# Hybrid mLSTM / sliding-window step: the last two row tiles in another order, the samples' decay on GpSimd, keys loaded ahead of queries

## The chip, the core and the metric

One core of a Trainium2 chip runs the whole program. The metric is the time of one execution on the device, in microseconds. The engines are TensorE (PE, with its weight loads as PEld), VectorE (DVE), ScalarE (ACT), GpSimd (POOL) and SyncE (SP), which issues most DMAs. Each engine works through its own list of instructions in order and waits on semaphores that other engines and DMAs raise.

## The reference, cut to what matters

One layer of a decoder for 1024 prompt rows (d = 1024) and 32 sample rows (8 sequences of 4 tokens). The input goes through an adaptive normalisation and one wide projection; two branches follow, a matrix memory (mLSTM, 4 heads) and a sliding-window attention (8 query heads, 2 key/value heads, window 128); gates merge them, an output product and a residual follow, then a normalisation of each row.

```python
# mLSTM, one chunk
C_new = decay[..., None, None] * C + jnp.einsum('bhs,bhsd,bhse->bhde', w_end, k, v)
n_new = decay[..., None] * n + jnp.einsum('bhs,bhsd->bhd', w_end, k)
...
u = jax.nn.sigmoid(gm) * (y_m @ w_mo) + jax.nn.sigmoid(ga) * (y_a @ w_ao)
x = x + gate * (u @ w_o)
...
# rmsnorm(yp, g_final), rmsnorm(ys, g_final)
y = xf * lax.rsqrt(jnp.mean(xf * xf, axis=-1, keepdims=True) + NORM_EPS) * g
```

All is in float32. For the samples, C is 128 x 128 for each of 8 sequences and 4 heads, and n one more column; the decay is one number for each sequence and head.

## The kernel before, in words

Every large product is made of three matmuls in a reduced float32 form (high by high, high by low, low by high), so each operand is split first: ACT casts the high part, DVE subtracts it to get the low part. The big products run as seven block products in place of eight (a scheme after Strassen), so sums and differences of blocks are made by DVE too.

The order of the work around the large products is planned when the program is written out. A class, Side, holds streams of smaller work: attention units (one for each of 4 query groups and 4 pairs of row tiles), memory heads, and the four sample heads. Each is a generator; where it yields, it names a number of microseconds of matmul time to wait and the PSUM banks it wants next, and Side takes it up again between matmuls. The matmuls, and most instructions of DVE and ACT, are held in the order in which they are written (Ordered, line 212); GpSimd and SP are ordered by the scheduler.

Three places matter here.

- **Attention unit** (unit, line 856). It loads queries (tile uqv, from the DRAM tensor qD), the keys of up to three row tiles (tile ukv, from kD) and values. A call of dma first writes out stores that are still due for the tensor it reads. Then come the scores (PSUM tile sc): the queries' slices are PE's weights, the keys are streamed.
- **Sample head** (sample_head, line 1205). For one head the eight sequences' C and n lie in three tiles Cs (three, three and two sequences of 129 columns). Matmuls into sn read them; then they are multiplied by the decay (line 1261, in sxb); matmuls into sU make the update, and DVE adds it to Cs. Columns 128 of Cs go back to n by GpSimd. Meanwhile the large products use the PSUM tiles bw, bx, by and bz in turn; zt is one of the gate tiles made from bx.
- **The end** (lines 2240 to 2332). The output product runs over four blocks of two row tiles (256 rows). For a block, the seven products go to the PSUM tiles X, Z, W and Y (foX, foZ, foW, foY in the trace). The splits of the seven left operands are u3wh and u3wl for the last block. xb holds two rows of residuals, tile 6 and tile 7 in the last block; all of them are slices of two large tiles that the trace calls rows_h and rows_l, and so are g_final (gf, with its sign turned) and the samples' rows (x8, y8). add_row adds a product to a slice of xb; square (ACT, with a sum of its output) gives the sums of squares, one column of ss (fss) for a half or quarter row; norm_sum adds the columns up and scales them (fv); root_recip makes the negative reciprocal root: a square root on ACT, then a reciprocal and one Newton step on DVE (fy, fw). weighted multiplies by g_final, rows_out scales by the root and stores to y_p. In the last block the two halves of Y are separate PSUM tiles of 256 columns, so that their additions can start sooner. A row tile of 128 x 1024 goes out as two stores of 256 KB.

Of the kernel before, what the change touches and what calls it, by code (L numbers as in the profile page):

```python
# [20 lines left out]
D = 1024  # L21
SEQ = 1024
NB = 8
# [150 lines left out]
def body(tc, a):  # L174
    nc = tc.nc
    with ExitStack() as ctx:
# [20 lines left out]
        def sm(shape, name, bufs=3, dt=F32):  # L197
            return sp.tile(shape, dt, tag=name, bufs=bufs, name=name)
# [55 lines left out]
        def dma(out, in_, late=False):  # L254
            stores(in_.tensor)
            issue(out, in_, late)
# [599 lines left out]
        def unit(g, b0):  # L856
# [3 lines left out]
            qv, kv_ = ht([128, 4, 128], "uqv"), ht([128, 4, 128], "ukv")  # L860
            q, kT = qv[:, 0:2].rearrange("p c e -> p (c e)"), kv_[:, 0:3].rearrange("p c e -> p (c e)")
            vn = kv_[:, 3], qv[:, 2], qv[:, 3]
            dma(q, qD[g][:, b0 * 128:b0 * 128 + 256])
            dma(kT[:, n0 * 128:], kD[:, (b0 - 1 + n0) * 128:(b0 + 2) * 128])
            dma(qv[:, 2:4], vnD[:, b0:b0 + 2])
            if b0:
                dma(vn[0], vnD[:, b0 - 1])
# [337 lines left out]
        def sample_head(h):  # L1205
# [52 lines left out]
                mm(num[j:j + 32], qf[:, b * NS:(b + 1) * NS], Cs[b // 3][:, b % 3], start=(b < 4), stop=(b >= 4 and j > 0))  # L1258
            mm(num[:NS], z[:, 257:289], z[:, 128:257], start=False, stop=True)
            S.copy(ns4, num)  # L1260
            for c, b, m in zip(Cs, bs, ns_):
                V.tensor_tensor(c[:, :m], c[:, :m], sxb[:, h, 2, b].unsqueeze(2).to_broadcast((128, m, 129)), op=ALU.mult)
            yield 4.0, "ob"
            for i, (c, b, m) in enumerate(zip(Cs, bs, ns_)):
                up = (pb, pb, po)[i]([128, 388], f"sU{h}_{i}")
# [868 lines left out]
        def row_start():  # L2134
            if order_out:
                i, n = order_out.pop(0)
                blocks_of_rows[i].start(n)
# [26 lines left out]
        def residual(tb):  # L2164
            xb = misc[3 + tb % 4]
            dma(xb, a["x_prompt"][tb * 128:tb * 128 + 128], tb < 4)
            return xb
# [12 lines left out]
        def norm_rows(ss, m, parts):  # L2180

            return root_recip(norm_sum(ss, m, parts), m)
# [13 lines left out]
        def square(x, ss):  # L2196
            S.activation(pb([128, 512], "sq")[:x.shape[0], :x.shape[1]], x, AF.Square, accum_out=ss)
# [42 lines left out]
        for i, r in enumerate(blocks_of_rows):  # L2240
            nxt = i < 3
            aside = lambda *when: next(rows8, None) if i in when else None
            before, xb, ss = (xb, ss), [residual(2 * i + c) for c in range(2)], sm([128, 6], "fss", 2)
            if not i:
                weights_out(len(wo_parts))
            X, Z = pg([128, 512], "foX"), pa([128, 512], "foZ")
            row_start()
            r.product(1, X, True)
            if i == 3:
                sum8 = pb([128, 512], "fo8s")[:, :1]  # L2250
                for j in range(4):
                    mm(sum8[32 * j:32 * j + 32], cst[:, C_S32:C_S32 + 32], sq8, start=True, stop=True, share=4)
            W = copied(X, "foW", pg, new=r.w[1] if i == 0 else None)
            if i:
                add_row(before[0][1], lo, Y[0])
            row_start()
            r.product(5, Z, True)
            if i == 3:
                V.memset(before[1][:, 5:6], 0.0)
                V.tensor_copy(before[1][:, 4:5], sum8)  # L2260
            if i:
                square(before[0][0][:, hi], before[1][:, 1:2])
                square(before[0][1][:, lo], before[1][:, 2:3])
                if not nxt:
                    for c, x in ((lo, 0), (hi, 1), (hi, 0), (lo, 1)):
                        weighted(before[0][x], c)
                rs = norm_rows(before[1], 2 if nxt else 3, 2)
            for x in xb:
                add_row(x, hi, Z)
            row_start()  # L2270
            r.product(6, W, False)
            parts = ((0, 512),) if nxt else ((0, 256), (256, 256))
            Y = [copied(W, f"foY{c0}", pb if c0 else pa, slice(c0, c0 + n), r.w[6] if c0 or i == 0 else None) for c0, n in parts]
            aside(1, 2)
            for c in range(2) if i else ():
                rows_out(2 * i - 2 + c, before[0][c], rs[:, c:c + 1], V if nxt else None)
            row_start()
            r.product(2, X, False)
            add_row(xb[0], lo, X)
            square(xb[0][:, lo], ss[:, 0:1])  # L2280

            def seventh():
                for y, (c0, n) in zip(Y, parts):
                    r.product(7, y, False, c0, n)
                    add_row(xb[1], slice(512 + c0, 512 + c0 + n), y)

            def first_row():
                r.product(3, W, False)
                add_row(xb[0], hi, W)

            if nxt:
                seventh()
                row_start()
                square(xb[1][:, hi], ss[:, 3:4])
                first_row()
                row_start()
                aside(0, 1, 2)
                if not i:
                    dma(gf, a["g_final"].to_broadcast((128, D)))
                    S.activation(gf, gf, AF.Copy, scale=-1.0)  # L2300
                elif i == 1:
                    dma(gs8, gsD)
                    for j in range(4):
                        dma(gf8[32 * j:32 * j + 32], a["g_final"][:, 256 * j:256 * j + 256].to_broadcast((32, 256)))
                    dma(x8, a["x_sample"])
                else:
                    S.activation(gf8, gf8, AF.Copy, scale=-1.0)
                row_start()
                r.product(4, Y[0], False)
            else:  # L2310
                first_row()
                V.scalar_tensor_tensor(y8, x8, rs[:, 2:3], gf8, op0=ALU.mult, op1=ALU.mult)
                issue(a["y_s"], y8)
                square(xb[0][:, hi], ss[:, 1:2])
                seventh()
                rs = norm_rows(ss, 1, 2)
                square(xb[1][:, hi], ss[:, 2:3])
                rows_out(6, xb[0], rs)
                y7 = ht([128, 512], "foy7")
                for f, (y, (c0, n)) in enumerate(zip(Y, parts)):  # L2320
                    r.product(4, y, False, c0, n)
                    c = slice(c0, c0 + n)
                    if f:
                        weighted(xb[1], hi)
                        half = norm_sum(ss[:, 2:4], 1, 2)
                        add_row(xb[1], c, y)
                        V.tensor_tensor_reduce(y7[:, c], xb[1][:, c], xb[1][:, c], 1.0, 0.0, ALU.mult, ALU.add, accum_out=ss[:, 4:5])
                        V.scalar_tensor_tensor(half, ss[:, 4:5], 0.5 / D, half, op0=ALU.mult, op1=ALU.add)
                    else:
                        add_row(xb[1], c, y)  # L2330
                        square(xb[1][:, c], ss[:, 3:4])
        rows_out(7, xb[1], root_recip(half, 1), S)


OUTS = {
# [72 lines left out]
```

## Time and profile before

| | |
|---|---|
| median of 3 runs | 820.4 us (820.26 to 821.0) |
| the profiled execution's own time | 821.22 us |
| its span, first to last instruction | 819.4 us |
| mean granted TensorE clock | 0.996 |
| last matmul to the end of the span | 7.8 us, in which DVE is busy 3.6 and ACT 1.4 |
| busy: PE / DVE / ACT / POOL | 804.3 / 603.0 / 418.8 / 48.7 us |
| DMA | 165.51 MB, mean 202 GB/s |

The span is what the trace shows. The time of an execution has some 1.8 us more around it. A row of the time line reads: start and length in us, engine, line, operation, output tile <- input tiles, shapes, how many were merged, and in brackets how long the engine had been idle and what ended that. Line 220 is the helper through which most DVE, ACT and POOL instructions go, so tiles tell more than lines. Where an operation's record overlaps the next one's start by some 0.08 us, the engine had begun the next while the last one's output drained.

### The profile page before, as it was taken

The numbers are of one execution on the slowest core, as the hardware profiler recorded it, in microseconds if no ns is written. First come the engines' busy times: TensorE is split into PE (matmuls) and PEld (weight loads), VectorE is DVE, ScalarE is ACT, GpSimd is POOL, SyncE is SP. The second block draws the span as 40 slices with busy tenths as digits, with TensorE's granted clock in tenths as the row PEclk, the third lists the DMA queues.
The fourth block names the chain that finished last, engine by engine and source line by source line (L and its number), as shares of the span: only waits on it lengthen the run. The fifth ranks groups of instructions, "written<-read, shape, count | busy, mean of one in ns | idle before, by whom it ended". The sixth has DMA issues, their size and how long they took to land. (4 is left out here: it accounts for less than half of the span.)

```text
span 819.4 us, 15145 instructions
## 1 busy us (share of the span) xinstructions
PE 804.3 (98%) x5162; PEld 667.4 (81%) x5162; DVE 603.0 (74%) x1518; ACT 418.8 (51%) x1021; POOL 48.7 (6%) x121
## 2 busy tenths in 40 slices
PE   8999999999999999999999999999999999999996
PEld 5779898888788878888888888788888779997775
DVE  4899886755755557475668889898668997876666
ACT  5664356655565564546556555554446652224334
POOL 0120000010000000000001011010002101000000
PEclk9999999999999999999999999999999999999999
DMA  9993856646545424537764685764436689647632
GB/s 353 363 348 113 252 158 217 175 151 218 172 140 163 130 85 153 164 140 241 253 214 152 236 264 192 260 213 143 145 106 210 199 304 376 234 145 275 206 104 110
DMA packets 113475, 165.51 MB, mean 202 GB/s; under 512 B 21185, under 2 KB 55745, under 8 KB 113365
## 3 DMA queue, kind: packets, MB, share of 16 engines
q1 hardware_dynamic: 107172, 152.74, 56.3%
q10 hardware_dynamic: 4752, 7.60, 2.5%
q0 software_dynamic: 1472, 4.20, 1.3%
q8 instruction: 41, 0.67, 0.4%
q14 instruction: 38, 0.30, 0.1%
HBM read 115.51 MB, written 50.00 MB: 202 GB/s over the span
## 5 line engine op out<-in xcount | busy, mean ns | idle before, releaser
L220 ACT ACTIVATE p<-p,nmx 128x256 f32<-128x256 f32 (+1 forms) x64 | 31.1, 486 | 18.9 <-DVE nmx L220 17.9
L220 DVE CUSTOM_DVE_ANT_0 p<-sc,cst,sink 128x256 f32<-128x256 f32 (+1 forms) x64 | 26.1, 463 | 9.1 <-PE sc L275 9.0
L275 PE MATMUL g_aq<-h_h,wh_aq 128*128 128x384 f32 (+1 forms) x96 | 32.4, 337 | 0.1
L275 PE MATMUL g_aq<-h_h,wl_aq 128*128 128x384 f32 (+1 forms) x96 | 30.9, 322 | 0.0
L275 PE MATMUL g_aq<-h_l,wh_aq 128*128 128x384 f32 (+1 forms) x96 | 30.8, 321 | 0.0
L275 PE MATMUL g_w_mo<-ym_l,wh_w_mo 128*128 128x384 f32 (+1 forms) x96 | 30.8, 321 | 0.0
L275 PE MATMUL g_w_mo<-ym_h,wh_w_mo 128*128 128x384 f32 (+1 forms) x96 | 30.8, 321 | 0.0
L275 PE MATMUL g_w_mo<-ym_l,wl_w_mo 128*128 128x384 f32 (+1 forms) x96 | 30.8, 321 | 0.0
L220 DVE COPY p<-pt 128x512 f32<-128x512 f32 (+1 forms) x16 | 10.5, 656 | 15.2 <-PE pt L280 15.2
L220 ACT CAST wosh<-wor 128x512 fp32r<-128x512 f32 x24 | 14.8, 621 | 13.1 <-DVE wor L220 12.3
L275 PEld LDWEIGHTS g_aq<-h_h,wh_aq 128*128 128x128 f32 x96 | 18.0, 188 | 2.8 <-issue 1.5
L261 POOL DMA_DIRECT2D oD<-uqv x16 | 8.9, 553 | 179.6 <-ACT uqv L220 164.1
L220 DVE TENSOR_TENSOR wosl<-wor,wosh 128x512 fp32r<-128x512 f32 x24 | 16.5, 686 | 3.9 <-ACT wosh L220 3.2
L275 PE MATMUL sc<-ukv,uqv 64*128 64x256 f32 (+1 forms) x128 | 18.0, 390 | 0.9 <-DMA ukv<-kD 0.9
L220 DVE SCALAR_TENSOR_TENSOR tgw_mo<-tgw_mo,g_w_mo 128x384 f32<-128x384 f32 (+1 forms) x24 | 12.4, 518 | 8.6 <-PE g_w_mo L275 6.4
L275 PEld LDWEIGHTS g_w_mo<-ym_l,wh_w_mo 128*128 128x128 f32 x96 | 18.0, 188 | 0.0
L275 PEld LDWEIGHTS g_aq<-h_l,wh_aq 128*128 128x128 f32 x96 | 18.1, 188 | 0.0
L275 PEld LDWEIGHTS g_w_mo<-ym_h,wh_w_mo 128*128 128x128 f32 x96 | 18.0, 188 | 0.0
L275 PEld LDWEIGHTS g_w_mo<-ym_l,wl_w_mo 128*128 128x128 f32 x96 | 18.0, 188 | 0.0
L275 PEld LDWEIGHTS g_aq<-h_h,wl_aq 128*128 128x128 f32 x96 | 18.0, 188 | 0.0
L220 DVE TENSOR_TENSOR et<-et,S 128x384 f32<-128x384 f32 (+1 forms) x12 | 6.1, 509 | 15.0 <-PE S L275 15.0
L275 PE MATMUL g_mq<-h_h,wh_mq 128*128 128x384 f32 (+1 forms) x48 | 16.7, 349 | 0.3 <-ACT mk L220 0.3
(2065 smaller groups left out, 2819.7 us busy)
## 6 DMA issues: line engine op xcount, KB each, us to landing
early_h<-w_ada SPq DMA_DIRECT2D x8, 512.0 KB
adar_ga<-w_ada SPq DMA_DIRECT2D x16, 256.0 KB
wr_ga<-w SPq DMA_DIRECT2D x16, 256.0 KB
wr_gm<-w SPq DMA_DIRECT2D x16, 256.0 KB
taD<-gt SPq DMA_DIRECT2D x16, 256.0 KB
tmD<-gt SPq DMA_DIRECT2D x16, 256.0 KB
wor<-w_out SPq DMA_DIRECT2D x16, 256.0 KB
tga<-taD SPq DMA_DIRECT2D x16, 256.0 KB
```

Of the source, the lines that this page charges most:

```text
L220: ins = f(*args, **kw)
L261: ins = (eng or nc.sync).dma_start(out, in_)
L275: in_order(nc.tensor.matmul(out, lhsT, rhs, start=start, stop=stop, skip_group_check=more))
```

## The change

The queries' and keys' loads of an attention unit trade places. The samples' decay becomes eight operations on GpSimd, one for each sequence (128 x 129, with one number for each partition), in place of three on DVE. At the end, the last block's second half is written out in another order: the split of the last left operand comes behind the addition of X; tile 6 is weighted on DVE before its root is known and scaled on ACT (scaled_half) in place of one DVE operation that did both; half of product 7 and a weighting stand between tile 6's root on ACT and its reciprocal; tile 7's four sums of squares and a constant column (EPS times D) are added by one reduction, and the root is taken from that sum, with half of it over D computed beside the root.

```diff
@@ unit
+            dma(kT[:, n0 * 128:], kD[:, (b0 - 1 + n0) * 128:(b0 + 2) * 128])
             dma(q, qD[g][:, b0 * 128:b0 * 128 + 256])
-            dma(kT[:, n0 * 128:], kD[:, (b0 - 1 + n0) * 128:(b0 + 2) * 128])
             dma(qv[:, 2:4], vnD[:, b0:b0 + 2])
@@ sample_head
             S.copy(ns4, num)
-            for c, b, m in zip(Cs, bs, ns_):
-                V.tensor_tensor(c[:, :m], c[:, :m], sxb[:, h, 2, b].unsqueeze(2).to_broadcast((128, m, 129)), op=ALU.mult)
+            for b in range(NB):
+                c = Cs[b // 3][:, b % 3]
+                G.tensor_scalar(c, c, sxb[:, h, 2, b:b + 1], None, op0=ALU.mult)
             yield 4.0, "ob"
@@ the blocks of rows
-            row_start()
+            if nxt:
+                row_start()
             r.product(2, X, False)
             add_row(xb[0], lo, X)
-            square(xb[0][:, lo], ss[:, 0:1])
+            if nxt:
+                square(xb[0][:, lo], ss[:, 0:1])
 
-            def seventh():
-                for y, (c0, n) in zip(Y, parts):
+            def seventh(ps=(0, 1)):
+                for y, (c0, n) in list(zip(Y, parts))[ps[0]:ps[-1] + 1]:
                     r.product(7, y, False, c0, n)
                     add_row(xb[1], slice(512 + c0, 512 + c0 + n), y)
...
-            else:
-                first_row()
-                V.scalar_tensor_tensor(y8, x8, rs[:, 2:3], gf8, op0=ALU.mult, op1=ALU.mult)
-                issue(a["y_s"], y8)
-                square(xb[0][:, hi], ss[:, 1:2])
-                seventh()
-                rs = norm_rows(ss, 1, 2)
-                square(xb[1][:, hi], ss[:, 2:3])
-                rows_out(6, xb[0], rs)
-                y7 = ht([128, 512], "foy7")
-                for f, (y, (c0, n)) in enumerate(zip(Y, parts)):
-                    r.product(4, y, False, c0, n)
-                    c = slice(c0, c0 + n)
-                    if f:
-                        weighted(xb[1], hi)
-                        half = norm_sum(ss[:, 2:4], 1, 2)
-                        add_row(xb[1], c, y)
-                        V.tensor_tensor_reduce(y7[:, c], xb[1][:, c], xb[1][:, c], 1.0, 0.0, ALU.mult, ALU.add, accum_out=ss[:, 4:5])
-                        V.scalar_tensor_tensor(half, ss[:, 4:5], 0.5 / D, half, op0=ALU.mult, op1=ALU.add)
-                    else:
-                        add_row(xb[1], c, y)
-                        square(xb[1][:, c], ss[:, 3:4])
-        rows_out(7, xb[1], root_recip(half, 1), S)
+
+        def scaled_half(tb, x, c, r):
+            S.activation(x[:, c], x[:, c], AF.Copy, scale=r)
+            issue(a["y_p"][tb * 128:tb * 128 + 128, c], x[:, c])
+
+        def rest_of_seventh():
+            weighted(xb[0], hi)
+            seventh((1,))
+            square(xb[1][:, 768:1024], ss[:, 3:4])
+
+        V.scalar_tensor_tensor(y8, x8, rs[:, 2:3], gf8, op0=ALU.mult, op1=ALU.mult)
+        issue(a["y_s"], y8)
+        row_start()
+        square(xb[0][:, lo], ss[:, 0:1])
+        first_row()
+        square(xb[0][:, hi], ss[:, 1:2])
+        weighted(xb[0], lo)
+        seventh((0,))
+        square(xb[1][:, 512:768], ss[:, 2:3])
+        V.memset(ss[:, 6:7], EPS * D)
+        r6 = root_recip(norm_sum(ss, 1, 2), 1, rest_of_seventh)
+        scaled_half(6, xb[0], hi, r6)
+        r.product(4, Y[0], False, 0, 256)
+        add_row(xb[1], slice(0, 256), Y[0])
+        square(xb[1][:, 0:256], ss[:, 4:5])
+        scaled_half(6, xb[0], lo, r6)
+        weighted(xb[1], hi)
+        r.product(4, Y[1], False, 256, 256)
+        add_row(xb[1], slice(256, 512), Y[1])
+        y7 = ht([128, 512], "foy7")
+        V.tensor_tensor_reduce(y7[:, 0:256], xb[1][:, 256:512], xb[1][:, 256:512], 1.0, 0.0, ALU.mult, ALU.add, accum_out=ss[:, 5:6])
+        v = sm([128, 3], "fv", 2)
+        V.tensor_reduce(v[:, 0:1], ss[:, 2:7], op=ALU.add, axis=AX.X)
+        r7, w = (sm([128, 4], n, 2)[:, :1] for n in ("fy", "fw"))
+        S.activation(r7, v[:, 0:1], AF.Sqrt, scale=1.0 / D)
+        V.tensor_scalar(v[:, 1:2], v[:, 0:1], 0.5 / D, None, op0=ALU.mult)
+        V.reciprocal(r7, r7)
+        V.scalar_tensor_tensor(w, r7, v[:, 1:2], r7, op0=ALU.mult, op1=ALU.mult)
+        V.scalar_tensor_tensor(r7, w, 1.5, r7, op0=ALU.subtract, op1=ALU.mult)
+        rows_out(7, xb[1], r7, S)
```

More of the change, by code (lines that the diff above doesn't have):

```diff
@@ L2242, in body @@
             aside = lambda *when: next(rows8, None) if i in when else None
-            before, xb, ss = (xb, ss), [residual(2 * i + c) for c in range(2)], sm([128, 6], "fss", 2)
+            before, xb, ss = (xb, ss), [residual(2 * i + c) for c in range(2)], sm([128, 7], "fss", 2)
             if not i:
```

## The prediction, made before the result was known

> **What bounds the kernel now.** I read the page first, then the waits of PE, then the end of the time line, engine by engine.
>
> ```profile
> span 819.4 us, 15145 instructions
> PE 804.3 (98%) x5162; PEld 667.4 (81%) x5162; DVE 603.0 (74%) x1518; ACT 418.8 (51%) x1021; POOL 48.7 (6%) x121
> ```
>
> PE is busy 98% of the span, so an edit on another engine pays only in two ways: it shortens a wait of PE, or it shortens the stretch after the last matmul. The view of waits (who waited for whom: us in total, times, longest) lists what PE lost to others. After the start-up these two are the longest:
>
> ```profile
> PE bx L275 <- DVE zt L220: 1.3, 1, 1.3
> PE sc L275 <- DMA ukv<-kD: 0.9, 1, 0.9
> ```
>
> The change touches both: the samples' decay stood ahead of zt on DVE, and ukv is the tile that the keys are loaded into. What else it touches is the end. Here is the time line from the last matmul on (start, length, engine):
>
> ```profile
> 811.31 0.28 PE L275 MATMUL foY<-wosh,u3wl 128*128 128x256 f32 x1
> ...
> 810.41 1.42 DVE L220 SCALAR_TENSOR_TENSOR rows_h<-rows_h,fy,rows_l 128x512 f32<-128x512 f32 x2
> 811.74 0.41 DVE L220 TENSOR_TENSOR rows_h<-rows_h,foY 128x256 f32<-128x256 f32 x1
> 812.08 0.69 DVE L220 TENSOR_TENSOR rows_h<-rows_h,rows_l 128x512 f32<-128x512 f32 x1
> ...
> 813.01 0.41 DVE L220 TENSOR_TENSOR rows_h<-rows_h,foY 128x256 f32<-128x256 f32 x1
> 813.46 0.42 DVE L220 CUSTOM_DVE_ANT_0 foy<-rows_h 128x256 f32<-128x256 f32 x1
> 813.93 0.16 DVE L220 SCALAR_TENSOR_TENSOR fv<-fss,fv 128x1 f32<-128x1 f32 x1
> 814.36 0.16 DVE L220 RECIPROCAL fy<-fy 128x1 f32<-128x1 f32 x1 [0.27 <-ACT fy L220]
> 815.00 0.75 DVE L220 SCALAR_TENSOR_TENSOR rows_h<-rows_h,fy,rows_l 128x512 f32<-128x512 f32 x1
> ```
>
> The last matmul ends at 811.59, but its sum is added only at 813.01: DVE was still busy scaling row tile 6 (810.41), weighting tile 7 (812.08) and adding partial sums (to 813.01). So 1.4 us of the tail are DVE's queue, not arithmetic that needs the last product. From 813.01 to the end all is one chain.
>
> **Term 1, the last two row tiles.** DVE's rows from the scaling of tile 6 on; rows_h holds both tiles, foY the last products' two halves. Before:
>
> ```order
> L220 SCALAR_TENSOR_TENSOR rows_h_8801<-rows_h_8801,fy,rows_l_8800 128x512 x2
> L220 TENSOR_TENSOR rows_h_8801<-rows_h_8801,foY_9418 128x256
> L220 TENSOR_TENSOR rows_h_8801<-rows_h_8801,rows_l_8800 128x512
> L220 TENSOR_SCALAR fv<-fss 128x1
> L220 SCALAR_TENSOR_TENSOR fv<-fss,fv 128x1
> L220 TENSOR_TENSOR rows_h_8801<-rows_h_8801,foY_9420 128x256
> L220 ISA foy_9508,fss<-rows_h_8801 128x256
> L220 ISA fss 128x1
> L220 SCALAR_TENSOR_TENSOR fv<-fss,fv 128x1
> ```
>
> and now:
>
> ```order
> L220 TENSOR_TENSOR rows_h_8821<-rows_h_8821,foY_9438 128x256
> L220 TENSOR_TENSOR rows_h_8821<-rows_h_8821,rows_l_8820 128x512
> L220 TENSOR_TENSOR rows_h_8821<-rows_h_8821,foY_9440 128x256
> L220 ISA foy_9562,fss<-rows_h_8821 128x256
> L220 ISA fss 128x1
> L220 TENSOR_REDUCE fv<-fss 128x1
> L220 TENSOR_SCALAR fv<-fv 128x1
> ```
>
> The two scalings of tile 6 have gone to ACT, the partial sums to one reduction behind the last square; only the weighting of tile 7 stands between the two additions. The weightings of tile 6 that replace the scalings on DVE moved up, into gaps:
>
> ```profile
> 803.52 0.68 DVE L220 TENSOR_TENSOR u3wl<-u_h,u3wh 128x512 fp32r<-128x512 f32 x1
> 805.65 0.69 DVE L220 TENSOR_TENSOR u3wl<-u_l,u3wh 128x512 fp32r<-128x512 f32 x1 [1.45 <-ACT u3wh L220]
> 806.26 0.68 DVE L220 TENSOR_TENSOR rows_h<-rows_h,foX 128x512 f32<-128x512 f32 x1
> 806.86 0.68 DVE L220 TENSOR_TENSOR rows_h<-rows_h,foW 128x512 f32<-128x512 f32 x1
> 807.46 0.47 DVE L220 SCALAR_TENSOR_TENSOR rows_l<-rows_l,fy 128x256 f32<-128x256 f32 x1
> 808.75 0.42 DVE L220 TENSOR_TENSOR rows_h<-rows_h,foY 128x256 f32<-128x256 f32 x1 [0.48 <-PE foY L275]
> ```
>
> A 512-wide DVE operation takes a slot of 0.60 (806.26 to 806.86). In the new order the addition of X (0.60) and the samples' output (0.40) fill the 1.45 us hole before 805.65. From there I step through: the addition of W at 806.26, a weighting at 806.86, first half of product 7 at 807.46, partial sums to 808.3, the other weighting to 808.9, second half of 7 to 809.25 (its matmuls end at 808.71), root of tile 6 done about 809.85. The first half of product 4 is added when PE ends it, 810.2, the weighting of tile 7 runs to 811.2, and DVE is idle when the last matmul ends. The last addition then starts 0.04 behind PE, as at 808.75 (matmuls to 808.71): at 811.63 instead of 813.01. Gain: **1.38 us**.
>
> Behind it the chain stays as long: addition, square, its read-out, one small DVE operation (a reduction over five columns in place of a 0.16 us operation, 813.93), root on ACT, reciprocal. The new 0.5/D product stands ahead of the reciprocal, but beside the root: 0.20 after the reduction against 0.43 from 813.93 to 814.36. It costs nothing while that cover lasts, 0.2 without it. ACT takes on two scalings:
>
> ```profile
> 812.25 0.39 ACT L220 ACTIVATE sq<-rows_h 128x256 f32<-128x256 f32 x1 [1.90 <-DVE rows_h L220]
> 814.12 0.20 ACT L220 ACTIVATE fy<-fv 128x1 f32<-128x1 f32 x1 [1.36 <-DVE fv L220]
> 815.00 0.72 ACT L220 ACTIVATE rows_h<-rows_h,fy 128x512 f32<-128x512 f32 x1 [0.68 <-DVE fy L220]
> ```
>
> At 0.72 each, with a square between: 809.9, 810.6 (square, read-out), 811.1 to 811.8. The root of tile 7 wants ACT at about 812.75, so 0.9 us of room. Bounds of this term: 1.38 if so, about 0.5 if ACT runs a whole scaling late. The store of tile 6 leaves SP at 811.9, about as before (behind 811.8), so the last store has the queue to itself.
>
> **Term 2, the samples' decay on GpSimd.** Only the third head's decay stands before a wait of PE. DVE and PE there:
>
> ```profile
> 526.03 0.68 DVE L220 TENSOR_TENSOR wl_pquery_gate__6563<-wr_az,wh_pquery_gate__6562 128x512 fp32r<-128x512 f32 x1
> 526.77 0.68 DVE L220 TENSOR_TENSOR ws<-wr_az,wr_az 128x512 f32<-128x512 f32 x1
> 527.58 1.36 DVE L220 TENSOR_TENSOR Cs<-Cs,sxb 128x387 f32<-128x387 f32 x3
> 528.86 0.68 DVE L220 TENSOR_TENSOR wr_az<-wr_az,wr_az 128x512 f32<-128x512 f32 x1
> 529.46 0.67 DVE L220 SCALAR_TENSOR_TENSOR zt<-zt,bx 128x512 f32<-128x512 f32 x1
> ...
> 525.12 0.62 PE L275 MATMUL sn<-Cs,qd 128*32 128x129 f32 x16
> 530.19 0.50 PE L275 MATMUL bx<-h_h,wh_pquery_gate__6469 128*128 128x512 f32 x1 [1.30 <-DVE zt L220]
> 532.39 0.63 PE L275 MATMUL sU<-vm,skn 96*128 96x388 f32 x3
> ```
>
> PE wants the bank bx back and waits 1.30 for zt. The three decays take 527.58 to 528.86, 1.28 us. But the scheduler put another operation ahead of zt. Before, from the two small sums on:
>
> ```order
> L220 TENSOR_TENSOR gts<-gts,osm 128x32 x2
> L220 TENSOR_TENSOR Cs_0_6339<-Cs_0_6339,sxb 128x387
> L220 TENSOR_TENSOR Cs_1_6340<-Cs_1_6340,sxb 128x387
> L220 TENSOR_TENSOR Cs_2_6341<-Cs_2_6341,sxb 128x258
> L220 TENSOR_TENSOR wr_az_0_6405<-wr_az_0_6401,wr_az_0_6405 128x512
> L220 SCALAR_TENSOR_TENSOR zt<-zt,bx 128x512
> ```
>
> and now:
>
> ```order
> L220 TENSOR_TENSOR gts<-gts,osm 128x32 x2
> L220 TENSOR_TENSOR wr_az_0_6415<-wr_az_0_6411,wr_az_0_6415 128x512
> L220 TENSOR_TENSOR wr_az_0_6411<-ws_6573,wr_az_0_6411 128x512
> L220 SCALAR_TENSOR_TENSOR zt<-zt,bx 128x512
> L220 TENSOR_TENSOR zt<-zt,ho 128x512
> ```
>
> So zt gains 1.28 and loses 0.60: 0.68. From this comes off what GpSimd, now at work at the same time, takes from DVE. The trace has such pairs:
>
> ```profile
> 35.09 0.24 POOL L220 CAST h_h<-small 128x64 fp32r<-128x64 f32 x1
> 20.94 0.62 POOL L220 CAST wh_av<-wr_av 128x512 fp32r<-128x512 f32 x1
> 621.47 1.40 POOL L220 TENSOR_TENSOR yat3l<-yr,yat3h 128x512 fp32r<-128x512 f32 x1 [3.15 <-ACT yat3h L220]
> ...
> 35.10 0.77 DVE L220 TENSOR_TENSOR h_l<-x,h_h 128x512 fp32r<-128x512 f32 x1 [0.23 <-ACT h_h L220]
> 621.75 1.66 DVE L220 TENSOR_TENSOR wr_mo<-wr_mo,wr_mo 128x512 f32<-128x512 f32 x1
> ```
>
> A DVE operation on two SBUF tensors takes 0.68 alone, 0.77 beside a one-input GpSimd operation of 64 columns, 1.66 beside a two-input one of 512. GpSimd's decay is one-input, 129 columns; scaled by columns from the first pair (0.08 for 64), 0.16 a meeting, and as little as 0, as much as 0.98 by the second. From about 525.6 to zt I count three full-size two-input operations that can be delayed (behind 526.03, behind 526.77, the second wr_az): 0.48. What is left is **0.20 us**, between 0.68 (no meeting costs) and a loss. The Trainium skill (GPSIMD Engine Reference, 4.1 Engine selection) calls one-input work on GpSimd roughly line-rate, which at that page's 1.2 GHz makes an estimate of 0.11 for 129 columns: three meetings at that price would take 0.33, and the whole prediction would be 818.35 in place of 818.5. The row above (0.77 against 0.69) says dearer, and I keep to it.
>
> Length on GpSimd: by the two casts about 0.30 for 129 columns, eight make 2.4, and with a DVE operation waited out each time about 5.5. From 525.6 that ends by 531.1, before the sum with sU (532.39). The other three heads' decays stand before no listed wait of PE, so I give them nothing.
>
> **Term 3, keys' loads first.** SP's queue at the first attention unit, as a piece of the difference:
>
> ```order
> -L261 DMA qD_114<-aqr 128x384 x2
> +L261 DMA qD_114<-aqr 128x384
> +L261 DMA ukv<-kD 128x256
> +L261 DMA qD_114<-aqr 128x384
>  L261 DMA qD_114<-aqr 128x256
>  L261 DMA uqv<-vnD 128x256
>  L261 DMA uqv<-qD_114 128x256
> -L261 DMA ukv<-kD 128x256
> ```
>
> ```profile
> SPq L261 <- DMA qD<-aqr: 3.3, 1, 3.3
> ...
> 84.37 1.42 SPq L261 DMA_DIRECT2D qD<-aqr  x3
> 89.72 0.32 SPq L261 DMA_DIRECT2D uqv<-qD  x1
> 90.09 0.42 SPq L261 DMA_DIRECT2D ukv<-kD  x1
> 92.34 0.93 PE L275 MATMUL sc<-ukv,uqv 64*128 64x128 f32 x8 [0.89 <-DMA ukv<-kD]
> ```
>
> SP holds the queries' load until the first store of the queries has landed (the wait of 3.3); the keys' load, which needs none of that, stood behind it, 0.37 later, and PE waited for it. Now it goes out five us early and the queries' load is last. Its own time doesn't move (the first store stays ahead of it), so with an equal flight PE starts 0.37 sooner. Between 0 (if the queries landed as late) and 0.89; I take **0.35**. In the other fifteen units no such wait is listed, so nothing.
>
> **The sum.** 1.38 + 0.20 + 0.35 = 1.93 us: the profiled execution's span goes from 819.4 to 817.5, its time by the same step from 821.2 to 819.3. The three runs have a median of 820.4, so I predict **818.5**. PE's later waits are round trips that begin at PE, so they move along.
>
> **Rivals.** A: only the tail pays; GpSimd's meetings eat the 0.68 and the queries land no sooner: 820.4 - 1.38 = 819.0. For it: the measured 0.77 and 1.66; against it: three meetings must cost 0.23 each. B: the meetings cost nothing: 820.4 - 1.38 - 0.68 - 0.35 = 818.0; for it, that a decay may fall beside work that reads PSUM, as zt does. C: the tail gives little, because ACT reaches the last root a scaling late: 820.4 - 0.5 - 0.55 = 819.35; against it, 0.9 us of room. D, the slower side: DVE's meetings with GpSimd before zt. GpSimd runs eight decays from 525.6 on, and if each DVE operation on two SBUF tensors in that stretch (the three, and the small sums counted as two) waits as long as in the two-input pair, 0.98, zt comes 4.9 - 0.68 = 4.2 later and PE with it: 820.4 - 1.73 + 4.2 = 822.9. Five meetings turn the whole change into a loss from 0.48 each. The page named above states the cause as well (1. Specifications: the SBUF interfaces are shared, with contention against instructions with two SBUF inputs), without a price, and the 1.66 agrees. Against D: GpSimd's one-input cast over 512 columns takes 0.62 in all, and a decay is a quarter as wide.
>
> **Chances.** Forecast (818.1 to 818.9) 0.50; A 0.20; B 0.13; C 0.11; D 0.06. What can't be told from no change is 0.2%, 1.6 us: faster means below 818.76, slower above 822.0. The forecast's case lies below that line in 0.45 of its 0.50, B wholly, A in 0.05: faster 0.63. Same: the rest of A and of the forecast, C, and the milder meetings of D: 0.33. Slower 0.04, the rest of D. Range 817.7 to 819.6: it leaves out D and the edges of B and C.
>
> **What would show it.** Tail: the last addition on DVE within 0.1 us of the last matmul's end, two ACT scalings ending before the last root, and some 7.8 - 1.4 = 6.4 us from the last matmul to the end. Decay: bx waits about 1.1 instead of 1.30, DVE's wl and ws rows around GpSimd's decays lengthened by 0.1 to 0.2. Keys: sc waits about 0.5, on uqv. I'm wrong if DVE rows there stretch to a microsecond, if ACT's square or scaling ends behind 812.7, or if PE finds a new wait.

## The result, and the profile after

| | before | after |
|---|---|---|
| median | 821.04 us (22 runs, 820.08 to 824.11) | 818.85 us (22 runs, 817.71 to 820.05) |
| ratio after / before | | 0.9971, 95% interval 0.9965 to 0.9977 |
| profiled execution, its span | 821.22, 819.4 us | 820.05, 818.3 us |
| the same two kernels later, beside other runs | 821.48 us (22 runs) | 818.59 us (10 runs), ratio 0.9965 (0.9954 to 0.9976) |

The change made the kernel 2.4 us faster by the ratio (0.0029 of 821.04; interval 1.9 to 2.9) and 2.2 by the two medians. Forecast were 818.5 us and 1.93 us of gain, reckoned from a median of 820.4 over three runs of the kernel before; over 22 runs that median is 821.04. So the time lies in the range and the sign is right. The gain is some 0.4 us larger than the sum gave, and the time is still 0.35 us above the forecast, since the kernel before is 0.6 us slower than was taken. By the line that the prediction drew at 818.76, 0.2% under 820.4, the time of 818.85 is just on the side of no change; beside the 821.04 measured with it, it is 0.29% shorter. The profiled execution of the change happens to be the slowest of its 22. Its span is only 1.1 us shorter than before's, and that needs an explanation of its own.

The view of PE's waits after the change (who waited for whom: us in total, times, longest), from the places that the prediction spoke of and one that it didn't:

```profile
PE sc L275 <- DMA uqv<-qD: 1.6, 1, 1.6
PE bx L275 <- DVE zt L220: 1.0, 1, 1.0
PE foW L275 <- DVE u0wl L220: 0.5, 1, 0.5
```

The wait of sc is now ended by the queries (uqv) and not by the keys, but it has grown from 0.89 to 1.55. The wait of bx has shrunk from 1.30 to 0.99. The wait of foW for u0wl, at 743 us, is new.

The time line of the end after the change:

```profile
809.86 0.72 ACT L220 ACTIVATE rows_h<-rows_h,fy 128x512 f32<-128x512 f32 x1
...
810.66 0.69 DVE L220 TENSOR_TENSOR rows_h<-rows_h,rows_l 128x512 f32<-128x512 f32 x1
...
811.25 0.71 ACT L220 ACTIVATE rows_h<-rows_h,fy 128x512 f32<-128x512 f32 x1
...
811.44 0.28 PE L275 MATMUL foY<-wosh,u3wl 128*128 128x256 f32 x1
...
811.75 0.42 DVE L220 TENSOR_TENSOR rows_h<-rows_h,foY 128x256 f32<-128x256 f32 x1 [0.41 <-PE foY L275]
812.21 0.43 DVE L220 CUSTOM_DVE_ANT_0 foy<-rows_h 128x256 f32<-128x256 f32 x1
812.56 0.08 DVE L220 DVE_READ_ACCUMULATOR2_ANT fss<- 128x1 f32 x1
812.75 0.16 DVE L220 TENSOR_REDUCE fv<-fss 128x1 f32<-128x5 f32 x1
812.94 0.20 ACT L220 ACTIVATE fy<-fv 128x1 f32<-128x1 f32 x1 [0.98 <-DVE fv L220]
...
813.17 0.17 DVE L220 RECIPROCAL fy<-fy 128x1 f32<-128x1 f32 x1
...
813.82 0.75 DVE L220 SCALAR_TENSOR_TENSOR rows_h<-rows_h,fy,rows_l 128x512 f32<-128x512 f32 x1
```

The last addition starts 0.03 us behind the last matmul's end (811.72), and DVE had been idle 0.41 us before it: nothing but PE holds it up. From the start of the last matmul to the start of the last scaling it is 2.38 us; before it was 3.69 (811.31 to 815.00). The two scalings of tile 6 on ACT end at 811.96, and ACT is then idle 0.98 us until the last root. From the last matmul's end to the end of the span, the last store included, it is 6.6 us; before it was 7.8, and 6.4 was forecast.

DVE, GpSimd and PE around zt in the third head:

```profile
525.03 6.59 POOL L220 TENSOR_SCALAR Cs<-Cs,sxb 128x129 f32<-128x129 f32 x8 [18.25 <-PE sn L275]
...
525.46 0.68 DVE L220 TENSOR_TENSOR wl_pquery_gate__6578<-wr_az,wh_pquery_gate__6577 128x512 fp32r<-128x512 f32 x1
...
526.20 0.78 DVE L220 TENSOR_TENSOR ws<-wr_az,wr_az 128x512 f32<-128x512 f32 x1
526.90 0.38 DVE L220 TENSOR_TENSOR gts<-gts,osm 128x32 f32<-128x32 f32 x2
527.20 0.68 DVE L220 TENSOR_TENSOR wr_az<-wr_az,wr_az 128x512 f32<-128x512 f32 x1
527.92 0.75 DVE L220 TENSOR_TENSOR wr_az<-ws,wr_az 128x512 f32<-128x512 f32 x1
528.58 0.68 DVE L220 SCALAR_TENSOR_TENSOR zt<-zt,bx 128x512 f32<-128x512 f32 x1
...
529.32 0.50 PE L275 MATMUL bx<-h_h,wh_pquery_gate__6479 128*128 128x512 f32 x1 [0.99 <-DVE zt L220]
...
531.51 0.65 PE L275 MATMUL sU<-vm,skn 96*128 96x388 f32 x3
531.96 1.03 DVE L220 TENSOR_TENSOR Cs<-Cs,sU 128x387 f32<-128x387 f32 x2 [0.73 <-PE sU L275]
```

From the start of the last wl split to zt it takes 3.12 us where it took 3.43 (526.03 to 529.46): the 0.31 that bx gained. DVE's rows are a little stretched (ws 0.78 and not 0.68). GpSimd needs 6.59 us for its eight decays; it is done at 531.62, only 0.34 us before DVE reads the result at 531.96.

### The profile page after: what moved, and what is told of

Same layout as the page of the kernel before. It is cut to its first block, busy times and chain, and to the rows that moved or that the text cites. A ratio compares the mean times of both kernels' runs of the same rounds, so it can differ in the third digit from the quotient of the medians.

```text
span 818.3 us, 15170 instructions
## 1 busy us (share of the span) xinstructions
PE 804.0 (98%) x5162; PEld 667.2 (82%) x5162; DVE 600.2 (73%) x1506; ACT 420.5 (51%) x1025; POOL 75.7 (9%) x153
## 5 line engine op out<-in xcount | busy, mean ns | idle before, releaser
L220 POOL TENSOR_SCALAR Cs<-Cs,sxb 128x129 f32<-128x129 f32 x32 | 27.0, 861 | 43.1 <-PE sn L275 43.1
```

What stands on the lines that cost most here:

```text
L220: ins = f(*args, **kw)
```

## The experiments

Each is told as its edit, what was expected of it, what was measured and what follows. The time of one kernel scatters by some 2 us from execution to execution, and the intervals of these ratios are 1.4 to 2.2 us wide. So terms of 0.3 us are read from the traces, and a table of all profiles stands at the end of this section.

**The tail alone.** The kernel before with the new order of the last two row tiles; the other two hunks of the diff left out.

> The kernel before with the new order of the last two row tiles alone; decay on VectorE and the order of the loads as before. The prediction's term: 1.38 us faster, the last addition within 0.1 us of the last matmul's end. By the trace of the whole change, where the stretch behind the last matmul went from 7.81 to 6.58 us: 1.2 to 1.3 us faster and nothing else moved, PE's waits up to 790 us the same as before. Rival: part of what the whole change gained at the end came from the other two edits, then the stretch stays above 6.9 us and the time falls by less than 0.9.

Measured: 820.16 us against 820.91, ratio 0.9986 (0.9977 to 0.9995): 1.1 us, between 0.4 and 1.9 (the two medians are only 0.75 apart). From the last matmul to the last scaling it is 2.38 us again, and bx waits 1.30 as before:

```profile
812.75 0.28 PE L275 MATMUL foY<-wosh,u3wl 128*128 128x256 f32 x1
813.07 0.42 DVE L220 TENSOR_TENSOR rows_h<-rows_h,foY 128x256 f32<-128x256 f32 x1 [0.41 <-PE foY L275]
815.13 0.75 DVE L220 SCALAR_TENSOR_TENSOR rows_h<-rows_h,fy,rows_l 128x512 f32<-128x512 f32 x1
```

So 1.31 us of the change come from the tail, and need neither of the other parts. In one thing the expectation failed: PE's waits were not those of before. It waited 1.9 us for sc and 0.4 for u0wl, with nothing changed ahead of either.

**The decay on GpSimd alone.**

```diff
-            for c, b, m in zip(Cs, bs, ns_):
-                V.tensor_tensor(c[:, :m], c[:, :m], sxb[:, h, 2, b].unsqueeze(2).to_broadcast((128, m, 129)), op=ALU.mult)
+            for b in range(NB):
+                c = Cs[b // 3][:, b % 3]
+                G.tensor_scalar(c, c, sxb[:, h, 2, b:b + 1], None, op0=ALU.mult)
```

> The kernel before with the samples' decay on GpSimd alone. Prediction: bx waits 1.10 in place of 1.30 us and the time falls by 0.20. By the trace of the whole change: bx waits about 1.0, a decay takes 0.6 to 0.9 us on GpSimd, and PE is 0.3 us ahead from there to 740 us. Two theories on what comes of this lead. Gate: VectorE's additions of the first residual rows at about 741 wait for loads that do not move with PE, the split of u0 stands behind them, so PE waits there for as long as it is ahead: 0.1 to 0.4 us for u0wl, and the time falls by less than 0.15. No gate: PE waits for nothing there, and the time falls by 0.3.

Measured: 820.6 us, ratio 0.9998 (0.999 to 1.0007), which can't tell 0.3 us from nothing. bx waits 1.00, u0wl 0.21. The wait for u0wl is in the bounds of the gate theory; but the run before had 0.42 of it with no lead at all, so the lead isn't its cause. That theory falls; what the wait is comes below.

**The keys' loads first, alone.** The two lines of the first hunk.

> The kernel before with the keys' loads ahead of the queries' alone. Prediction: the first sc starts 0.37 us sooner after the issue of the queries' load than before (2.25 in place of 2.62 us), the wait falls from 0.89 to about 0.5, the time by 0.35. Rival: the queries' load, now with the three modulation loads right behind it instead of the keys' load, takes longer itself (the trace of the whole change had 3.36 us from its issue to sc): 2.6 to 3.4 us, and no gain, or a loss up to 0.7. In both cases the gate at 741 us takes up to 0.4 us of what is gained.

Measured: 820.47 us, ratio 0.9995 (0.9987 to 1.0004). The time line has:

```profile
88.89 0.32 SPq L261 DMA_DIRECT2D uqv<-qD  x1
...
91.20 0.93 PE L275 MATMUL sc<-ukv,uqv 64*128 64x128 f32 x8 [0.53 <-DMA uqv<-qD]
```

2.31 us from the issue to sc, and 0.53 of wait: what the prediction said, and not the 3.36 of the change's first profile. One of the two is chance, or both.

**No decay at all.** The kernel before without the decay's two lines.

> The kernel before with the samples' decay left out altogether (the samples' state is summed undecayed, so its outputs are other numbers); VectorE has the same order of instructions as with the decay on GpSimd. It tells how much of the missing gain is contention. If the prediction's count is right (1.28 off VectorE, 0.60 for the operation that moved ahead), bx waits 0.62 us here, and what the run with GpSimd's decay waits more is what GpSimd takes from VectorE (0.37 by the trace of the whole change, 0.48 by the prediction). Rival: no contention, the order or an earlier operation sets zt: bx waits about 1.0 here too.

Measured: 820.66 us, ratio 0.9997 (0.9987 to 1.0007). In the same order of DVE's instructions as with GpSimd's decay:

```profile
528.05 0.68 DVE L220 TENSOR_TENSOR wl_pquery_gate__6554<-wr_az,wh_pquery_gate__6553 128x512 fp32r<-128x512 f32 x1
...
528.78 0.69 DVE L220 TENSOR_TENSOR ws<-wr_az,wr_az 128x512 f32<-128x512 f32 x1
529.38 0.29 DVE L220 TENSOR_TENSOR gts<-gts,osm 128x32 f32<-128x32 f32 x2
529.59 0.69 DVE L220 TENSOR_TENSOR wr_az<-wr_az,wr_az 128x512 f32<-128x512 f32 x1
530.31 0.69 DVE L220 TENSOR_TENSOR wr_az<-ws,wr_az 128x512 f32<-128x512 f32 x1
530.92 0.68 DVE L220 SCALAR_TENSOR_TENSOR zt<-zt,bx 128x512 f32<-128x512 f32 x1
...
531.65 0.50 PE L275 MATMUL bx<-h_h,wh_pquery_gate__6463 128*128 128x512 f32 x1 [0.74 <-DVE zt L220]
```

From wl to zt 2.87 us, against 3.12 with GpSimd at work and 3.43 before. So GpSimd takes 0.25 us from DVE here, in three places of 0.06 to 0.1 each (ws 0.78 for 0.69, the two small sums 0.38 for 0.29, the second wr_az 0.75 for 0.69; the first wr_az loses nothing), and what the decay's move is worth without that is 0.56.

**The decay on ACT.** The changed kernel with

```diff
-                G.tensor_scalar(c, c, sxb[:, h, 2, b:b + 1], None, op0=ALU.mult)
+                S.activation(c, c, AF.Copy, scale=sxb[:, h, 2, b:b + 1])
```

> The changed kernel with the samples' decay on ACT instead of GpSimd, eight scalings of 129 columns a head. Without the decay bx waited 0.74 us, with it on GpSimd 1.00. If GpSimd's cost to VectorE is what lies between, bx waits 0.7 to 0.8 us here, VectorE's ws row is back at 0.69 (0.78) and PE is 0.25 us further ahead from 531 us on. Rival: ACT's eight scalings (about 0.25 us each, 2 us a head) make the casts of the next gate weights late, and VectorE's differences and PE behind them: a wait that the others do not have, bx at 1.0 or more.

Measured: 818.09 us (6 runs) against 821.11, ratio 0.9967 (0.9956 to 0.9979); bx waits 0.74, as without any decay. That shows in a second way that the 0.25 us is GpSimd's contention: with the work done on an engine that leaves DVE alone, it goes. Casts on ACT made nothing late, though one scaling takes 0.40 us and not 0.25 (32 of them, min / median / max in ns):

```profile
L220 ACT ACTIVATE Cs<-Cs,sxb x32: 387/398/420, 459.3 to 548.7; 128x129 f32<-128x129 f32 x32
```

**Three wide decays on GpSimd.** The kernel before, with one factor for each tile Cs:

```diff
+                f = c[:, :m].rearrange("p b e -> p (b e)")
+                G.tensor_scalar(f, f, sxb[:, h, 2, b][:, 0:1], None, op0=ALU.mult)
```

> The kernel before with the decay on GpSimd as three operations of 387, 387 and 258 columns, each with one factor for all its sequences (other numbers in the samples' state). It measures what sets the 0.61 us of a decay of 129 columns where 0.30 was predicted. If it is a price by the instruction, the wide ones take 0.9 to 1.1 us and the three together under 3.2 us; if it goes by columns (4.7 ns each), 1.8 us for 387 and 4.9 us for the three.

The same view of GpSimd's decays, first of the changed kernel and then of this one:

```profile
L220 POOL TENSOR_SCALAR Cs<-Cs,sxb x32: 605/802/1322, 460.4 to 554.2; 128x129 f32<-128x129 f32 x32
```

```profile
L220 POOL TENSOR_SCALAR Cs<-Cs,sxb x12: 1069/1429/2309, 460.9 to 551.6; 128x387 f32<-128x387 f32 x8, 128x258 f32<-128x258 f32 x4
```

At the least, 129 columns take 0.61 us, 258 columns 1.07 and 387 columns 1.26. That makes 2.5 to 3.6 ns a column and 0.1 to 0.3 us an instruction, so the price lies between the two expectations. Three wide ones took 3.9 to 5.9 us a head and eight small ones 6.0 to 7.8: fewer and larger ones save a quarter or more of GpSimd's time. But they hold DVE up more: bx waits 1.26 here, 0.52 above the run without a decay, twice the eight small ones' 0.25. (One run, 822.01 us.)

**The first residual rows loaded earlier.** In the order of SP's loads at 730 us, the residuals of row tiles 0 and 1 ahead of four loads of w_out, once on the changed kernel and once on the kernel before:

```diff
         rows8 = sample_rows()
+        first = [residual(c) for c in range(2)]
         next(rows8)
@@ the blocks of rows, at the loop's head
-            before, xb, ss = (xb, ss), [residual(2 * i + c) for c in range(2)], sm([128, 7], "fss", 2)
+            before, xb, ss = (xb, ss), [residual(2 * i + c) for c in range(2)] if i else first, sm([128, 7], "fss", 2)
```

> The changed kernel with one edit more: the loads of the first two residual row tiles leave SP ahead of the four loads of the samples' output weights. In the profiles so far PE waited for u0wl at about 743 us: 0, 0.51, 0.42, 0.21, 0.23, 0.38 us, whether or not PE was ahead upstream, since the additions of these rows wait for their load. Theory (a gate that a load's landing sets, a little different in every execution): the additions no longer end VectorE's idle time 6 to 7 us after the load's issue, the wait for u0wl is gone (under 0.1), and the time is 0.2 to 0.5 under the changed kernel's, some 2.6 to 2.9 under before. Rival (the stall only moves): the output weights, now 2.5 us later, are late for the samples' products at about 745.6 us, PE waits there, and nothing is gained.

> The kernel before with the residual loads first and nothing else. If the wait for u0wl comes in most executions of the kernel before too (its profile happened to show none, the tail alone showed 0.42), this gains 0.2 to 0.5 us on its own and u0wl waits under 0.1. If the gate only catches PE when the change has brought it ahead, it gains nothing.

Measured: 817.82 us (5 runs, ratio 0.9967, 0.9955 to 0.998) on the changed kernel, 820.77 (11 runs, ratio 1.0002, 0.9992 to 1.0012) on the one before. The wait for u0wl is gone in both profiles, as expected, and PE waits for nothing at the samples' products, so the rival of a stall that only moves is not borne out there; the times don't show the gain, and 0.2 to 0.5 us can't be excluded by them either. What the wait was, the changed kernel's own profile tells:

```profile
733.53 0.33 SPq L261 DMA_DIRECT2D rows_l<-x_prompt  x1
734.18 0.33 SPq L261 DMA_DIRECT2D rows_h<-x_prompt  x1
...
740.70 0.69 DVE L220 TENSOR_TENSOR rows_l<-rows_l,foZ 128x512 f32<-128x512 f32 x1 [6.44 <-DMA rows_l<-x_prompt]
741.87 0.69 DVE L220 TENSOR_TENSOR rows_h<-rows_h,foZ 128x512 f32<-128x512 f32 x1 [0.48 <-DMA rows_h<-x_prompt]
742.47 1.29 DVE L220 TENSOR_TENSOR u0wl<-u_l,u0wh 128x512 fp32r<-128x512 f32 x2
...
743.21 0.50 PE L275 MATMUL foW<-wo_b22h,u0wl 128*128 128x512 f32 x1 [0.51 <-DVE u0wl L220]
```

The same place in the profile of before, where the load took 6.7 us and PE came just as the first half of the split was done:

```profile
740.58 0.69 DVE L220 TENSOR_TENSOR rows_l<-rows_l,foZ 128x512 f32<-128x512 f32 x1 [5.78 <-DMA rows_l<-x_prompt]
...
742.34 1.29 DVE L220 TENSOR_TENSOR u0wl<-u_l,u0wh 128x512 fp32r<-128x512 f32 x2
...
743.09 0.49 PE L275 MATMUL foW<-wo_b22h,u0wl 128*128 128x512 f32 x1
```

In the changed kernel's profile DVE stands idle for 6.44 us at an addition whose rows land 7.2 us after their issue; u0wl is split behind the second addition, and PE is there first. With the residuals ahead of w_out in the queue, the second addition comes 1.7 us earlier (97.31 in place of 99.00 us after the start of the aw matmul at 643 that had waited) and PE waits for nothing there. One part of the expectation failed: DVE still waits 1.5 to 1.9 us for the rows of the second addition in the three profiles with this edit, only early enough for PE. And in the profile of the changed kernel with this edit PE lost 0.9 at another place, 653 us, which lies ahead of the edit:

```profile
PE az L275 <- DVE wl_ao1A L220: 0.9, 1, 0.9
```

That wait ends on DVE too, but it also hangs on a load: in this profile ACT's casts into ym_l, ahead of wl_ao1A in the chain, waited 0.65 and 0.87 us for the load of yr from ymD. In the change's first profile they waited 0.53 there, and PE lost some 0.3; in its second they waited for nothing, and neither did PE.

**The changed kernel once more, and the two variants beside it on one chip.**

> The changed kernel once more, beside the next two on the same chip. Its first profile was the slowest of 22 executions. What the profiles so far give by their parts: 1.31 us from the last matmul to the last scaling (2.38 in place of 3.69), 0.31 at bx, and at the first sc what the old order waited more on average than the new (1.55 and 0.85 us), 0.7: 2.3 us under before in the median. By the prediction's own terms 1.9. In this profile bx waits 0.99, u0wl between 0.2 and 0.6, and sc is released by uqv, not ukv.

> The changed kernel with the decay on ACT, beside the changed kernel. Theory (GpSimd takes 0.25 us from VectorE ahead of zt, and ACT has room for 3.2 us of scalings a head): bx waits 0.74 and the median is 0.25 us under the changed kernel's. Rival (its first profile was early by luck, with no wait for sc at all): medians equal within 0.1.

> The changed kernel with the decay on ACT and the residual loads ahead of the output weights. If the two gains are real and add up: bx waits 0.74, nothing waits for u0wl, and the median is 0.25 + 0.35 = 0.6 us under the changed kernel's. If the wait for u0wl only moves to another load (one of two profiles with residuals first had a wait of 0.91 at 653 us, ahead of the edit, which may be chance): no better than with the decay on ACT alone.

Measured, against 821.48 us of before: the changed kernel 818.59 (ratio 0.9965, 0.9954 to 0.9976), with the decay on ACT 818.61 (0.9966, 0.9956 to 0.9977), with the decay on ACT and the residuals first 818.48 (0.9961, 0.9947 to 0.9974). Both variants did in the profile what they should (bx 0.75 and 0.74; in the last one no wait for u0wl), and neither is measurably faster than the change. The medians are what the rival of the second expectation said, equal within 0.1, and not the 0.25 and 0.6 us of the theories; with intervals of some 2 us the times exclude neither, so these gains are seen in rows alone. The changed kernel itself was 2.9 us under before this time (2.0 to 3.8), where 2.3 and 1.9 had been put down; the wait for u0wl that was expected in its profile did not come. No version here beats it by more than its times scatter.

The changed kernel's second profile has a span of 816.8 us in place of 818.3, with the same program:

```profile
89.18 0.32 SPq L261 DMA_DIRECT2D uqv<-qD  x1
...
91.34 0.93 PE L275 MATMUL sc<-ukv,uqv 64*128 64x128 f32 x8 [0.36 <-DMA uqv<-qD]
```

sc starts 2.16 us after the queries' issue (3.36 in the first profile), and PE doesn't wait for u0wl. These two places make 1.2 and 0.7 us of difference, small losses at 653 us another 0.3, and the stretch up to the queries' issue made 0.7 the other way; the span differs by 1.5.

**All profiles.** For each, from its rows: the wait of sc; the time from the issue of the queries' load to sc; the waits of bx and of foW for u0wl; the time from the start of the aw matmul that had waited, at about 643 us, to fo8s at about 794; and the time from the last matmul's start to the last scaling's.

| kernel | sc waits | queries' issue to sc | bx waits | u0wl waited for | aw to fo8s | last matmul to last scaling |
|---|---|---|---|---|---|---|
| before | 0.89 | 2.62 | 1.30 | none | 150.59 | 3.69 |
| wide decays on GpSimd | 0.86 | 2.63 | 1.26 | 0.60 | 151.64 | 3.69 |
| tail alone | 1.89 | 3.95 | 1.30 | 0.42 | 151.60 | 2.38 |
| decay alone | 1.48 | 3.92 | 1.00 | 0.21 | 150.93 | 3.70 |
| no decay | 1.81 | 3.58 | 0.74 | 0.38 | 151.73 | 3.70 |
| before, residuals first | 2.35 | 4.12 | 1.30 | none | 150.52 | 3.70 |
| keys alone | 0.53 | 2.31 | 1.31 | 0.23 | 150.96 | 3.69 |
| the change | 1.55 | 3.36 | 0.99 | 0.51 | 151.59 | 2.38 |
| the change, second profile | 0.37 | 2.16 | 0.99 | none | 150.60 | 2.38 |
| decay on ACT | none | 2.17 | 0.74 | 0.36 | 151.46 | 2.38 |
| decay on ACT, second profile | 0.39 | 2.16 | 0.75 | 0.45 | 151.44 | 2.38 |
| the change, residuals first | 1.31 | 3.59 | 0.99 | none | 151.70 | 2.38 |
| decay on ACT, residuals first | 1.63 | 3.43 | 0.74 | none | 150.43 | 2.38 |

Two columns are the same to 0.02 us wherever the code is the same: bx and the tail. They are arithmetic on engines. The other columns are draws, that is, they differ from execution to execution of the same code. The queries' load comes in a short and a long form whatever the kernel: with the keys behind it 2.62 and 2.63, or 3.58 to 4.12; with the keys ahead 2.16 to 2.31, or 3.36 to 3.59. And with w_out ahead of the residuals, PE waits for u0wl in eight of ten profiles, by 0.2 to 0.6, and is then 0.3 to 1.2 us longer from aw to fo8s (the losses at 653 us are in it); with the residuals first in none of three.

## Why the prediction was right

**Term 1, the tail: right, mis-sized by 0.07.** 1.38 forecast, 1.31 measured, in every one of seven profiles. The step on the queue was exact: the last addition came 1.39 us nearer to the last matmul's start (0.31 behind it, and not 1.70). The step that failed is "behind it the chain stays as long": from the addition to the last scaling it takes 2.07 and not 1.99 us, since the reduction over five columns starts 0.54 behind the square (812.21 to 812.75), where the 0.16 us operation that it replaced started 0.47 behind it (813.46 to 813.93). Read it as a longer wait for the square's read-out, not as a longer operation: both take 0.16. The 0.5/D product beside the root cost nothing, as said. ACT's scalings came at 809.86 and 811.25, within 0.2 of the forecast, with 0.98 us to spare. Rival C, a late ACT, is out.

**Term 2, the decay: right in sign and place, mis-sized by 0.11 (0.20 forecast, 0.31 measured).** Two of its numbers were wrong and partly cancelled. Without contention the move is worth 0.56, not 0.68: the operation that the scheduler moved ahead of zt costs 0.72, not 0.60. With it the slot of the first wr_az grows to 0.72 (529.59 to 530.31 in the run without decay), and the operation that now follows, which overwrites a tile that this one reads, starts only at its end (530.28). And three meetings with GpSimd cost 0.25 and not 0.48, so a meeting with a 129-column decay is 0.06 to 0.10 and not 0.16. The three places are not quite those that were counted: the first wr_az lost nothing, and the two small sums, which the forecast did not count, lost 0.09. The pair from which I scaled, 0.08 for 64 columns, was nearer as it stood, unscaled. The estimate by the line rate of the Trainium skill (GPSIMD Engine Reference, 4.1 Engine selection) was 0.11 us for a decay of 129 columns and so 0.33 for three meetings; 0.25 measured is nearer to that than to mine. But its step on the way there, a decay as long as its columns at line rate, does not hold in the trace: 0.61 us.

The length of the decays was wrong by a factor of two: 0.30 each forecast, 0.61 at the least (eleven of the 32 take 0.61 to 0.62) and 0.86 on average measured, 6.59 us for the eight in place of 2.4 to 5.5. The step that failed took a cast's price by columns for a multiplication by one number for each partition. It did not decide, but the margin to DVE's sum with sU was 0.34 us and not the 1.3 that I had counted. Rival D (0.98 a meeting) is out by a factor of ten, rival B (no cost) by 0.25 us.

**Term 3, keys first: right.** Forecast were 0.35 us, a wait of about 0.5 on uqv. In like draws the gain is 0.43 (short: 2.63 to 2.20 on average; long: 3.89 to 3.46), and in the three profiles of the new order where PE waited on a short draw it waited 0.53, 0.37 and 0.39, on uqv. What failed is "with an equal flight": flights are equal only on average of draws. The first profile of the change drew the long form, so that alone would have read as a loss of 0.7, and as rival A. Over all profiles the new order starts 0.73 earlier after the issue (3.47 to 2.74), because four of its seven draws are short and two of the old order's six; whether the order makes short draws likelier, or that is chance, stays open. The explanation on record for a long one, the modulation loads right behind the queries, was not borne out: these loads follow as closely in the short draws.

**"PE's later waits are round trips that begin at PE, so they move along": wrong in the way it was put.** The wait for u0wl at 743 us hangs on the landing of a load, 6.6 to 7.3 us after its issue. It didn't show in the profile of before, where PE and the load met by chance, and so it was taken for no wait at all. A new wait of PE was named as a sign of being wrong, and the first profile of the change has one; the step that failed is that what ends PE's later waits was taken to begin at PE, where this one begins at a load's issue. I first read it in the change's profile as the place where the lead of 0.9 us was swallowed; the tail alone, with no lead, waited 0.42 and so took that reading away, and the change's second profile kept its whole lead and waited for nothing.

**The sum.** 1.31 + 0.31 + 0.43 = 2.05 us by the traces' like rows, 1.93 forecast, 2.4 (1.9 to 2.9) by the times. The time came within 0.35 us of 818.5 partly by luck: the kernel before was 0.6 us slower than its three runs had said, the gain 0.4 larger, and the two errors go against each other. Rival A's time, 819.0, lies near the measured one too, but its gain of 1.38 us is outside the interval. The time of the whole alone doesn't tell the forecast from rival B (2.41 us); the rows do, by the 0.25 us that GpSimd takes. The three parts alone gave 1.1, 0.2 and 0.4 in time, together 1.7. That the times gave 0.3 more than the rows is within their interval, and isn't explained further. Compared draw for draw, the profile of before and the second of the change (both with a short flight and no wait for u0wl) have spans of 819.4 and 816.8: of these 2.6 us, 1.31 are the tail, 0.31 bx, 0.52 sc with the start-up's rest, and 0.48 lies ahead of 50 us, where the programs are the same.

## What to carry to other kernels

Before a term of a few tenths is read from one profile, follow the chain behind the wait back to its start, and ask whether a load stands in it. Here the waits with engines alone behind them (bx, the tail) repeated to hundredths of a microsecond; those with a load behind them were draws, even where the last link was DVE (u0wl, wl_ao1A), and the queries' flights lay some 1.3 us apart. Such a wait wants several profiles, sorted into like ones. The chain of small operations at the end was not shortened by merging its links (it became 0.08 us longer); what paid was to take work out of the queue ahead of it. Work moved to GpSimd was cheap for DVE in small pieces (0.06 to 0.1 us a meeting) but slow in itself, and ACT, which had the room, did the same scaling without any cost to DVE.

## What the runs showed of the hardware that was not expected

- A multiplication by one number for each partition takes GpSimd 0.61 us for 128 x 129 float32, as long as its cast of 128 x 512 (0.62). ACT takes 0.40 for it, eight of them 3.2 us, where DVE's three operations did all eight in 1.28.
- GpSimd and DVE get along better than a lock for whole instructions would let them. The Trainium skill (SBUF — State Buffer, Who interferes with whom) says that a DVE operation with two SBUF inputs contends with a GpSimd operation that reads SBUF, and calls the contention an exclusive lock. In the third head GpSimd's decays run back to back from 525.03 to 531.62, 0.61 to 1.32 us each, and no DVE operation on two SBUF tensors up to zt is longer by more than 0.1 us (in the other heads 0.87 for 0.69 is the longest). That is not a wait of DVE for whole decays, and the measurement decides. GpSimd loses more: its decays stretch from 0.61 to as much as 1.32. With three times wider operations DVE's loss doubles (0.52 for 0.25).
- The queries' load has two flights, about 1.3 us apart (2.2 and 3.5, or 2.6 and 3.9 with the keys behind it). In all seven long draws, and in two of the six short ones, the view of DMA traffic shows a packet of the instruction queue in the same few microseconds (in one of these two it comes only after sc has started):

```profile
q8 instruction: 1, 0.02, 1.7%
```

  That is the changed kernel's first profile, from 0.5 us ahead of the queries' issue to 4 us behind it (packets, MB, share of the 16 DMA engines' time); the change's second profile and that of before have no such row there. Whether fetching instructions delays the load, or both follow from something else, was not tried.
